# The next expert's up product ahead of the down product, combines across row groups, and the overflow branch after the eighth expert

## The chip, the core and the metric

The kernel runs on one core of a Trainium2 chip. The metric is the device time of one execution in microseconds, the median of several runs; lower is better. Engines are named as in the profile: PE is TensorE (PEld its weight loads), DVE is VectorE, ACT is ScalarE, POOL is GpSimd, and SP is the engine whose queue issues the weight loads. TensorE's clock has two levels here, 1.2 and 2.4 GHz; the profile gives the granted clock as a share of the higher one.

## The reference, cut to what matters

Two transformer blocks follow each other on 256 tokens of width 1024. The first has a mixer (mLSTM and sparse attention) and then a mixture of experts; the second has differential attention, a recurrent branch and a dense feed-forward part, twice. The change concerns the experts alone:

```python
logits = h @ w_router + b_router                 # 256 tokens, 32 experts
vals, idx = top_k(logits, 4); gate = softmax(vals)
for each expert e, for the tokens that chose it:
    up = x @ w_up[e] + b_up[e]                   # 1024 -> 2048
    glu, lin = split(up, 2)
    glu = min(glu, 7); lin = clip(lin, -7, 7)
    act = glu * sigmoid(1.702 * glu) * (lin + 1)
    out[token] += gate * (act @ w_down[e] + b_down[e])   # 1024 -> 1024
```

All of it is in fp32. The weights of one expert are 12 MiB, those of all 32 experts 403 MB; every expert is computed, with its own tokens only.

## The kernel before

**Stages.** The mixer and the router come first. At line 1131 `moe` runs the experts, `after_moe` (line 1334) normalises the sum and adds it to the residual, and `block2` (line 1473) runs the second block with weights that `load2` (line 1381) loads. The order of instructions on each engine comes from a scheduling pass, which mostly keeps program order but lets an instruction go earlier where it expects its engine to be idle.

**Slots and order.** An expert is given a fixed number of token slots. Experts 0 and 1 have 64. The others are sorted by how many tokens chose them (`sort_experts`, line 1011): four heavy ones with 96 slots, fourteen middle ones with 64, twelve small ones with 32. They run as the string `mshmmhmshmmhms` says, after 0 and 1: m is a group of two middle experts, s one of four small ones, h one heavy expert. So the ninth expert is the first heavy one, and from it on there is a run of eight: heavy, middle, middle, middle, middle, heavy, middle, middle; the same run comes once more after the next four small ones. Tokens beyond an expert's slots go to `overflow` (line 1192), four loops that run only under `tc.If(over > 0)` (line 1188); with these inputs the branch isn't taken.

**Loads.** Each expert's weights are six loads of 2 MiB, two for the up product (the glu half), two for the linear product and two for the down product. `next_w` (line 1081) puts them in turn into eight buffers, so a load waits until PE has used the load eight places before. All go through SP's queue, in program order: up, linear, down, then the next expert.

**One expert** (`expert`, line 1242). With m slots, 128/m column blocks of the weights are computed at once, each into its own 32 or 64 output rows; a heavy expert is three blocks of 32 slots. In program order on PE: transposes of the gate matrix (`ps_pg`, L1265), the up product (`ps_u`, L1278, bias L1282), the linear product (`ps_l`), the first half of the work left over from the expert before, transposes of the activations (`ps_at`, L1307; ACT copies them, L1308), the second half of that work, and the down product (`ps_d`), which ACT copies to `y` (L1319). The left-over work is the combine of the expert before and, where a group ends, the gather of the next group's tokens (`ps_g`, L1234, whose one-hot columns DVE makes at L1222 and whose result ACT scales at L1236).

**Combine** (L1326, added to `acc` by DVE at L1329). The outputs `y` lie in 128/m row groups, one for each column block; a matmul with the gate matrix of a group gives that block's columns for all tokens. There is one closure for each group (middle experts: for each group and half of the tokens), and each goes through all its matmuls, in its own accumulation bank, before the next begins. The eight banks (`ps`) serve every product, gather and transpose as well. An fp32 matmul shows as two records in the trace.

**The end.** After the last expert its combine runs, then `load2(0, 0, NW)` issues the first four loads of block 2, then comes the branch, then the other loads of block 2. `after_moe` follows with high priority: transposes of x into four banks (L1355), squares (L1346, L1347), a Newton rsqrt on DVE and a diagonal (L1360), and the matmuls at L1368; meanwhile the first weights of block 2 are split into two parts (ACT L1392, DVE L1395).

Of the kernel before, what the change touches and what calls it, by code (L numbers as in the profile page):

```python
# [19 lines left out]
P = 128  # L20
# [17 lines left out]
LEAD1 = 3  # L38
NFF = DFF // P
# [154 lines left out]
class Kernel:  # L194
# [936 lines left out]
    def moe(self):  # L1131
# [9 lines left out]
        ahead, todo = {}, []  # L1141
        with ExitStack() as s:
# [7 lines left out]
            for r in order:  # L1150
                if r == 0:
                    w = self.w01
                elif r == 1:
                    src = self.expert_chunks(1)
                    w = [self.next_w(src[c], f"we1_{c}") for c in range(6)]
                else:
                    reg = nc.sync.value_load(self.eord[0:1, r : r + 1], min_val=0, max_val=NE - 1)
                    src = self.expert_chunks(reg)
                    w = [self.next_w(src[c], f"we{r}_{c}") for c in range(6)]
                n = slots[r]  # L1160
                if r < 2:
                    col = col01[r]
                    if r == 0:
                        x01, steps = self.gather(col01, 64, "01")
                        for f in steps:
                            f()
                    xg = x01[:, :, r * 64 : r * 64 + 64]
                else:
                    col = (self.sslot[:, :, r : r + 1], self.sgate[:, :, r : r + 1], self.perm3[:, r : r + 1])
                    xg = ahead[r]  # L1170

                i = order.index(r) + 1
                if i < NE and order[i] in after and order[i] > 1:
                    g = after[order[i]]
                    m = slots[g[0]]
                    xs, steps = self.gather([(self.sslot[:, :, q : q + 1],) for q in g], m, f"{g[0]}")
                    for j, q in enumerate(g):
                        ahead[q] = xs[:, :, j * m : j * m + m]
                    todo += steps
                todo = self.expert(col, n, w, xg, f"{r}", (lambda: self.sort_experts(pm)) if r == 0 else None, todo)  # L1180
                if r == 0:
                    over = nc.values_load(self.rem[0:1, NE : NE + 1], min_val=-T1, max_val=T1)
                    self.consts2(self.kp)
            for f in todo:
                f()
            self.wx = None
            self.load2(0, 0, NW)
            with tc.If(over > 0):
                self.overflow()
            self.load2(0, NW)  # L1190

    def overflow(self):
# [5 lines left out]
        for lo, hi, cap in ((0, 2, 64), (2, 2 + NHEAVY, 96), (2 + NHEAVY, NE - NSMALL, 64), (NE - NSMALL, NE, 32)):  # L1198
            with tc.For_i(lo, hi, 1) as r:
                for b in range(-(-(T1 - cap) // 64)):  # L1200
                    rem = nc.values_load(self.rem[0:1, bass.ds(r, 1)], min_val=-T1, max_val=T1)
                    with tc.If(rem > 64 * b):
# [9 lines left out]
                        for f in self.expert((cslot, cgate, cperm), 64, w, xg, f"o{lo}_{b}"):  # L1212
                            f()
# [28 lines left out]
    def expert(self, col, n, w, xg, tag, between=None, fill=()):  # L1242
# [8 lines left out]
        per = 512 // wd  # L1251
        wide = [min(per, u - i) * wd for i in range(0, u, per)]
# [3 lines left out]
        gt = []  # L1256
        for b in range(u):
            pg = pm.tile([P, 2, P], F32, name=f"pg{tag}_{b}", tag="pg", bufs=2)
            io = self.iotas[:, b * m : b * m + m].unsqueeze(1).to_broadcast([P, q, m])
            for tt in range(2):  # L1260
                o = pg[:, tt].rearrange("p (a b) -> p a b", b=m)
                nc.vector.tensor_scalar(o, io, slot[:, tt], gate[:, tt], op0=ALU.is_equal, op1=ALU.mult)  # L1262
            ppg = self.ps(f"ps_pg{tag}_{b}")
            for tt in range(2):
                nc.tensor.transpose(ppg[:, tt * P : tt * P + P], pg[:, tt], self.ident)  # L1265
# [720 lines left out]
```

## Time and profile before

| | us |
|---|---|
| median of 3 runs | 1983.63 |
| lowest and highest of them | 1977.98, 1987.27 |
| profiled execution, its own time | 1976.5 |
| span of that execution's trace | 1974.8 |
| PE busy in the span | 1804.5 (91%) |
| DVE, ACT, POOL busy | 817.0, 572.5, 263.1 |
| mean granted TensorE clock | 0.937 |

The page's second part cuts the span into 40 slices of 49.4 us. A timeline line gives start, duration, engine, line, operation and, in brackets, how long the engine had been idle before and what ended that. A count of records can be a little low, since some matmul records are missing. A suffix q (SPq, DVEq) means the engine's sequencer: branches, semaphores and the issue of loads.

### The profile page before, as it was taken

Reading aid. Unit: us, or ns where it says so; the run is one execution under the profiler, and the core shown is the slowest. Engines: PE = TensorE matmul, PEld = TensorE weight load, DVE = VectorE, ACT = ScalarE, POOL = GpSimd, SP = SyncE. Lnnn points to the kernel's source line nnn. Section 1 sums busy time; section 2 is a strip of 40 time slices with the busy share of each in tenths; the row PEclk is TensorE's granted clock in tenths of the full one; section 3 lists DMA queues with packets and bytes.
Section 4 is the critical chain, followed back from the end, with each engine's and each line's share of the span. In section 5 each row is a group of like instructions: output and inputs, shape, how many; then the busy total and the mean of one; then the engine's idle time right before and its main releaser. Section 6 shows DMA issues by size and latency. Waiting matters only on the chain. (4 is left out here: it accounts for less than half of the span.)

```text
span 1974.8 us, 34249 instructions
## 1 busy us (share of the span) xinstructions
PE 1804.5 (91%) x14547; PEld 1282.8 (65%) x14548; DVE 817.0 (41%) x1804; ACT 572.5 (29%) x1128; POOL 263.1 (13%) x259
## 2 busy tenths in 40 slices
PE   6999979968999998699999975879999999789998
PEld 3777743435543544354345433868999999689998
DVE  3364642211212122111222222687666557876653
ACT  3454611101111101010111101345444446354442
POOL 2213110000000000000000000151233202423320
PEclk8899989987989999898999987789999999899999
DMA  9447779999999989999998899221343453225441
GB/s 386 174 190 273 294 279 429 427 427 425 427 428 428 372 367 425 427 426 428 426 427 339 369 427 399 91 86 43 129 171 144 151 209 122 86 76 186 183 147 52
DMA packets 42698, 557.73 MB, mean 282 GB/s; under 512 B 4788, under 2 KB 5964, under 8 KB 8360
## 3 DMA queue, kind: packets, MB, share of 16 engines
q1 hardware_dynamic: 39920, 548.67, 68.0%
q0 software_dynamic: 1200, 4.29, 0.6%
q10 hardware_dynamic: 1416, 2.49, 0.4%
q8 instruction: 116, 1.90, 0.4%
q14 instruction: 46, 0.38, 0.1%
HBM read 554.37 MB, written 1.06 MB: 281 GB/s over the span
## 5 line engine op out<-in xcount | busy, mean ns | idle before, releaser
L338 PE MATMUL ps_lin<-xhi,wh 128*128 128x272 f32 (+1 forms) x1024 | 301.1, 295 | 1.5 <-ACT xhi L1373 1.5
L339 PE MATMUL ps_lin<-xlo,wh 128*128 128x272 f32 (+1 forms) x1024 | 297.2, 291 | 0.9 <-DVE xlo L1374 0.9
L340 PE MATMUL ps_lin<-xhi,wl 128*128 128x272 f32 (+1 forms) x1024 | 296.8, 290 | 0.0
L1278 PE MATMUL ps_u<-we,xg 128*32 128x256 f32 (+1 forms) x2048 | 215.0, 460 | 29.1 <-DMA we<-wexp 29.1
L1278 PE MATMUL ps_d<-we,at 128*32 128x256 f32 (+1 forms) x2048 | 215.6, 457 | 14.6 <-DMA we<-wexp 11.1
L1278 PE MATMUL ps_l<-we,xg 128*32 128x256 f32 (+1 forms) x2048 | 208.7, 447 | 20.6 <-DMA we<-wexp 20.6
L338 PEld LDWEIGHTS ps_lin<-xhi,wh 128*128 128x128 f32 x1024 | 197.2, 193 | 4.0 <-ACT xhi L1373 1.7
L339 PEld LDWEIGHTS ps_lin<-xlo,wh 128*128 128x128 f32 x1024 | 196.9, 192 | 1.4 <-DVE xlo L1374 1.1
L340 PEld LDWEIGHTS ps_lin<-xhi,wl 128*128 128x128 f32 x1024 | 197.0, 192 | 0.0
L1278 PEld LDWEIGHTS ps_u<-we,xg 128*32 128x32 f32 (+1 forms) x2048 | 88.3, 122 | 137.2 <-issue 92.3
L1278 PEld LDWEIGHTS ps_l<-we,xg 128*32 128x32 f32 (+1 forms) x2048 | 88.6, 120 | 129.4 <-issue 91.3
L1278 PEld LDWEIGHTS ps_d<-we,at 128*32 128x32 f32 (+1 forms) x2048 | 87.0, 121 | 130.0 <-issue 86.2
L1326 PE MATMUL ps_c<-y,gt 32*128 32x256 f32 (+1 forms) x512 | 133.7, 494 | 0.5 <-ACT y L1319 0.5
L1349 POOL TENSOR_TENSOR hT<-hT,g 128x1024 f32<-128x1024 f32 x1 | 3.2, 3249 | 972.9 <-DVE ssm L1347 972.9
L1329 DVE TENSOR_TENSOR hT<-hT,ps_c 128x512 f32<-128x512 f32 x128 | 83.7, 685 | 118.4 <-PE ps_c L1326 118.2
L1392 ACT CAST wh<-wgu 128x1024 fp32r<-128x1024 f32 x88 | 92.2, 1049 | 122.0 <-PE ps_lin L339 119.3
L1395 DVE TENSOR_TENSOR wl<-wgu,wh 128x1024 fp32r<-128x1024 f32 x88 | 108.3, 1231 | 41.2 <-ACT wh L1392 41.0
L1290 DVE TENSOR_SCALAR gl<-ps_u 128x512 f32<-128x512 f32 (+1 forms) x36 | 20.3, 572 | 241.8 <-PE ps_u L1282 241.8
L1262 DVE TENSOR_SCALAR pg<-cols,sslot,sgate 128x128 f32<-128x128 f32 x76 | 22.5, 344 | 204.2 <-PE ps_pg L1265 204.2
L1326 PEld LDWEIGHTS ps_c<-y,gt 32*128 32x128 f32 (+1 forms) x512 | 74.7, 210 | 41.5 <-issue 31.1
L1308 ACT COPY at<-ps_at 128x512 f32<-128x512 f32 (+1 forms) x36 | 17.3, 492 | 290.2 <-PE ps_at L1307 290.2
L338 PE MATMUL ps_lin<-ahi,wh 128*128 128x272 f32 (+1 forms) x352 | 100.5, 286 | 0.0
(675 smaller groups left out, 3078.5 us busy)
## 6 DMA issues: line engine op xcount, KB each, us to landing
we<-wexp SPq DMA_DIRECT2D x192, 2048.0 KB, 17.4
wgu<-wgu SPq DMA_DIRECT2D x22, 2048.0 KB, 7.8
win<-win SPq DMA_DIRECT2D x14, 2048.0 KB, 8.3
wada<-wada SPq DMA_DIRECT2D x12, 2048.0 KB, 8.3
wdn<-wdn SPq DMA_DIRECT2D x16, 1408.0 KB, 6.2
wout<-wout SPq DMA_DIRECT2D x6, 2048.0 KB, 7.8
wint<-wint SPq DMA_DIRECT2D x2, 2048.0 KB, 11.3
wcmpNone<-wcmp SPq DMA_DIRECT2D x1, 2048.0 KB, 24.3
```

The source lines that it names most:

```text
L338: nc.tensor.matmul(po[:m, :nn], hi[:, a], xh[k], start=(k == 0), stop=False)
L339: nc.tensor.matmul(po[:m, :nn], hi[:, a], xl[k], start=False, stop=False)
L340: nc.tensor.matmul(po[:m, :nn], lo[:, a], xh[k], start=False, stop=(k == nk - 1))
L1262: nc.vector.tensor_scalar(o, io, slot[:, tt], gate[:, tt], op0=ALU.is_equal, op1=ALU.mult)
L1278: nc.tensor.matmul(dst[b][s], lhs(k, b), ws[k // 4][:, o : o + wd], start=(k == 0 and b % per == 0), stop=False)
L1290: nc.vector.tensor_scalar(gl[i], pu[i], 7.0, 0.5, op0=ALU.min, op1=ALU.mult)
L1308: nc.scalar.copy(at[i], pt[:, :x])
L1326: nc.tensor.matmul(pc[:, (tt - t0) * wd : (tt - t0) * wd + wd], gt[b][rows[s], tt * P : tt * P + P], y[b // per][rows[s], (b % per) * wd : ...
L1329: nc.vector.tensor_tensor(a, a, pc.rearrange("p (a b) -> p a b", a=per), op=ALU.add)
L1349: nc.gpsimd.tensor_tensor(u[1], acc[:, 1], self.g2, op=ALU.mult)
L1392: nc.scalar.copy(hi, src)
L1395: nc.vector.tensor_tensor(lo, src, hi.bitcast(F32), op=ALU.subtract)
```

## The change

1. `expert` returns four steps, `up`, `lin`, `down` and `combine`. The gate transposes move from ahead of the up product to ahead of the linear one.
2. `moe` runs for each expert: its linear product, the combine of the expert before, then (where a new group begins) the gather and in any case the up product of the next expert, and only then its own transposes and down product. Loads are issued in that order too: linear, next up, down.
3. In the combine the loop over row groups is the innermost one: a matmul of each group in turn, each into its own bank; the adds on DVE follow when all are issued.
4. After the eighth expert (`NBREAK = 8`) the next up product is not brought forward. The eighth expert's combine runs, the ninth's six loads are issued, and then comes the branch with `overflow` inside. The loads inside it no longer advance the ring. The ninth expert starts behind it with its gather.
5. At the end the last combine is followed by `load2(0)` whole, with no branch in between.

The sort and `consts2` (constants of block 2) come after the first expert's up product; before, the sort stood there and the constants after its down product.

```diff
-        self.nw += 1
+        self.nw += not second
...
+            xg, last = {}, None
+            for n, r in enumerate(order):
+                nxt = order[n + 1] if n + 1 < NE else None
+                if r not in steps:
+                    for f in fetch(after[r]) if r in after else []:
+                        f()
+                    up(r)
+                if n == 0:
+                    self.sort_experts(pm)
                     over = nc.values_load(self.rem[0:1, NE : NE + 1], min_val=-T1, max_val=T1)
                     self.consts2(self.kp)
-            for f in todo:
-                f()
+                weights(r, 1)
+                steps[r][1]()
+                if last is not None:
+                    steps[last][3]()
+                last = r
+                ahead = nxt is not None and n + 1 != NBREAK
+                if ahead:
+                    weights(nxt, 0)
+                    for f in fetch(after[nxt]) if nxt in after else []:
+                        f()
+                    up(nxt)
+                weights(r, 2)
+                steps[r][2]()
+                if n + 1 == NBREAK:
+
+                    steps[last][3]()
+                    last = None
+                    for i in range(3):
+                        weights(nxt, i)
+                    with tc.If(over > 0):
+                        self.overflow()
+            steps[last][3]()
             self.wx = None
-            self.load2(0, 0, NW)
-            with tc.If(over > 0):
-                self.overflow()
-            self.load2(0, NW)
+            self.load2(0)
...
+        def combine():
+            gt, y = S["gt"], S["y"]
+
+            for t0 in range(0, 2, per):
+                pc = [self.ps(f"ps_c{tag}_{t0}{s}") for s in range(q)]
                 for tt in range(t0, t0 + per):
                     for b in range(u):
-                        nc.tensor.matmul(pc[:, (tt - t0) * wd : (tt - t0) * wd + wd], gt[b][rows[s], tt * P : tt * P + P],
-                                         y[b // per][rows[s], (b % per) * wd : (b % per) * wd + wd], start=(b == 0), stop=(b == u - 1))
-                a = self.acc[:, t0 : t0 + per, s * wd : s * wd + wd]
-                nc.vector.tensor_tensor(a, a, pc.rearrange("p (a b) -> p a b", a=per), op=ALU.add)
-            return f
-
-        return [combine(s, t0) for s in range(q) for t0 in range(0, 2, per)]
+                        for s in range(q):
+                            nc.tensor.matmul(pc[s][:, (tt - t0) * wd : (tt - t0) * wd + wd], gt[b][rows[s], tt * P : tt * P + P],
+                                             y[b // per][rows[s], (b % per) * wd : (b % per) * wd + wd], start=(b == 0), stop=(b == u - 1))
+                for s in range(q):
+                    a = self.acc[:, t0 : t0 + per, s * wd : s * wd + wd]
+                    nc.vector.tensor_tensor(a, a, pc[s].rearrange("p (a b) -> p a b", a=per), op=ALU.add)
+
+        return up, lin, down, combine
```

`weights(r, i)` issues the two loads of product i of expert r, if they are not issued yet; `fetch` starts a group's gather and returns its parts; `up(r)` makes the four steps of expert r and runs the first.

## Rows read from the trace of the kernel before

**Rows 1.** The page: bytes moved in each of 40 slices of 49.4 us.

```profile
GB/s 386 174 190 273 294 279 429 427 427 425 427 428 428 372 367 425 427 426 428 426 427 339 369 427 399 91 86 43 129 171 144 151 209 122 86 76 186 183 147 52
```

**Rows 2.** Stretches: busy time by engine (instructions), then PE clock, DMA share, GB/s.

```profile
540.00:550.00 10.00, 10.00 (x31) 7.69 (x29) 1.38 (x2) 0.59 (x1) 0.00 (x0) 0.53 1.00 424
...
660.00:740.00 80.00, 80.00 (x667) 39.83 (x660) 16.21 (x30) 8.34 (x20) 0.00 (x0) 0.96 0.87 357
...
1030.00:1115.00 85.00, 85.00 (x655) 43.55 (x648) 16.42 (x28) 8.31 (x19) 0.00 (x0) 0.92 0.84 342
...
1213.00:1232.00 19.00, 10.80 (x84) 8.15 (x84) 3.67 (x7) 5.49 (x8) 0.00 (x0) 0.64 0.96 403
```

**Rows 3.** The page, DMA issues: count, KB each, us from issue to landing.

```profile
win<-win SPq DMA_DIRECT2D x14, 2048.0 KB, 8.3
```

**Rows 4.** Timeline of PE at expert 0: start, us, [idle before].

```profile
285.69 0.66 PE L1307 MATMUL ps_at<-ident,li 128*128 128x128 f32 x4 [1.51 <-DVE li L1301]
...
287.02 7.09 PE L1278 MATMUL ps_d<-we,at 128*64 128x512 f32 x32 [0.68 <-ACT at L1308]
```

**Rows 5.** Timeline of PE, from the eighth expert to the seventeenth.

```profile
467.82 1.13 PE L1326 MATMUL ps_c<-y,gt 32*128 32x256 f32 x4
...
468.88 7.07 PE L1234 MATMUL ps_g<-oh,x 128*128 128x96 f32 x32
...
479.58 0.65 PE L1265 MATMUL ps_pg<-ident,pg 128*128 128x128 f32 x4
...
506.63 3.84 PE L1234 MATMUL ps_g<-oh,x 128*128 128x128 f32 x32
...
535.91 4.69 PE L1326 MATMUL ps_c<-y,gt 32*128 32x256 f32 x24
...
541.54 9.06 PE L1326 MATMUL ps_c<-y,gt 32*128 32x256 f32 x24
...
574.29 1.98 PE L1326 MATMUL ps_c<-y,gt 64*128 64x512 f32 x6
...
576.79 1.12 PE L1326 MATMUL ps_c<-y,gt 64*128 64x512 f32 x2
...
603.54 1.98 PE L1326 MATMUL ps_c<-y,gt 64*128 64x512 f32 x4
...
677.19 10.57 PE L1278 MATMUL ps_d<-we,at 128*32 128x256 f32 x192
...
707.91 5.86 PE L1326 MATMUL ps_c<-y,gt 32*128 32x256 f32 x24
...
752.35 0.44 PE L1265 MATMUL ps_pg<-ident,pg 128*128 128x128 f32 x2
```

**Rows 6.** Timeline of all engines around the end of the expert stage.

```profile
1213.16 3.53 PE L1278 MATMUL ps_d<-we,at 128*32 128x256 f32 x32 [2.88 <-SPq L1188]
...
1217.34 1.17 PE L1326 MATMUL ps_c<-y,gt 32*128 32x256 f32 x16 [0.53 <-ACT y L1319]
...
1218.50 2.48 DVE L1329 TENSOR_TENSOR hT<-hT,ps_c 128x512 f32<-128x512 f32 x4 [9.24 <-PE ps_c L1326]
...
1225.54 5.99 PE L1355 MATMUL ps_x<-ident,x 128*128 128x128 f32 x32 [7.03 <-DVEq L1188]
...
1226.76 3.87 ACT L1392 CAST wh<-win 128x1024 fp32r<-128x1024 f32 x4
...
1230.81 1.23 DVE L1347 CUSTOM_DVE_ANT_0 xlo<-hT 128x1024 fp32r<-128x1024 f32 x1 [9.83 <-ACT wh L1392]
...
1238.02 2.07 PE L1368 MATMUL ps_x<-ssm,um 128*128 128x128 f32 x8 [6.49 <-DVE ssm L1360]
```

**Rows 7.** The branch's instructions: count, duration min/median/max in ns, first and last start.

```profile
L1188 SPq EVENT_SEMAPHORE  x7: 17/17/17, 1211.0 to 1223.8; - x7
...
L1188 PEldq COMPARE_BRANCH  x1: 6066/6066/6066, 1218.0 to 1218.0; - x1
...
L1188 DVEq EVENT_SEMAPHORE  x2: 21/21/21, 1225.4 to 1230.5; - x2
```

More of the change, by code (lines that the diff above doesn't have):

```diff
@@ new lines, in moe, with weights, fetch @@
+            srcs, ws, steps = {}, {0: self.w01}, {}
+            def weights(r, i):
+                if r not in srcs:
+                    e = r if r < 2 else nc.sync.value_load(self.eord[0:1, r : r + 1], min_val=0, max_val=NE - 1)
+                    srcs[r] = self.expert_chunks(e)
+                w = ws.setdefault(r, [])
+                if len(w) <= 2 * i:
+                    w += [self.next_w(srcs[r][c], f"we{r}_{c}") for c in (2 * i, 2 * i + 1)]
+            def fetch(g):
+                n = slots[g[0]]
+                if g == [0]:
+                    xs, todo = self.gather(col01, n, "01")
+                    both = (0, 1)
+                elif g == [1]:
+                    return []
+                else:
+                    xs, todo = self.gather([(self.sslot[:, :, q : q + 1],) for q in g], n, f"{g[0]}")
+                    both = g
+                for i, q in enumerate(both):
+                    xg[q] = xs[:, :, i * n : i * n + n]
+                return todo
@@ L1240, in gather, with expert @@
         return xg, [part(k0) for k0 in range(0, KT, per)]
-    def expert(self, col, n, w, xg, tag, between=None, fill=()):
+    def expert(self, col, n, w, xg, tag):
         nc, pm = self.nc, self.pm
@@ L1254, in expert @@
         sel = perm.to_broadcast([96, m])
[L1256 to L1265, printed above, removed]
[L1266 to L1267 removed]
         rows = [slice(i * m, i * m + m) for i in range(q)]
+        xs = lambda k, b: xg[:, k, b * m : b * m + m]
+        S = {}
         def product(lhs, ws, boff, name):
@@ L1309, in expert, with up @@
-        for f in fill[half:]:
-            f()
-        def acts(k, b):
-            o = (b % per) * wd + (k % nt) * P + m * (k // nt)
-            return at[b // per][:, o : o + m]
-        py = product(acts, w[4:6], 2048, f"ps_d{tag}")
-        y = t("y")
-        for i in range(len(wide)):
-            nc.scalar.copy(y[i], py[i])
-        def combine(s, t0):
-            def f():
-                pc = self.ps(f"ps_c{tag}_{t0}{s}")
+        def up():
+            pu = product(xs, w(0), 0, f"ps_u{tag}")
+            gl, sg = t("gl"), t("sg", 3)
+            for i in range(len(wide)):
+                nc.vector.tensor_scalar(gl[i], pu[i], 7.0, 0.5, op0=ALU.min, op1=ALU.mult)
+                nc.scalar.activation(sg[i], gl[i], AF.Tanh, scale=1.702)
+                nc.vector.scalar_tensor_tensor(sg[i], sg[i], 1.0, gl[i], op0=ALU.add, op1=ALU.mult)
+            S["sg"] = sg
@@ new lines, in down, with acts @@
+        def down():
+            at, li = t("at"), S["li"]
+            for i, x in enumerate(wide):
+                pt = self.ps(f"ps_at{tag}_{i}")
+                for c in range(x // P):
+                    nc.tensor.transpose(pt[:, c * P : c * P + P], li[i][:, c * P : c * P + P], self.ident)
+                nc.scalar.copy(at[i], pt[:, :x])
+            def acts(k, b):
+                o = (b % per) * wd + (k % nt) * P + m * (k // nt)
+                return at[b // per][:, o : o + m]
+            py = product(acts, w(2), 2048, f"ps_d{tag}")
+            y = S["y"] = t("y")
+            for i in range(len(wide)):
+                nc.scalar.copy(y[i], py[i])
```

83 lines of the change are left out of this document (26 added, 57 removed).

## The prediction

> **What bounds the kernel now.** I read the page's forty slices first, for the stage in which experts run, then a table of stretches, the page's row of loads, the timeline of PE (TensorE) through the start and one run of experts, then the tail, and last the rows of the branch. The slices show the expert stage as the plateau of some 427 GB/s in slices 7 to 24 [rows 1]. Each load of 2 MiB then takes 2.097 MB / 427 GB/s = 4.91 us, and an expert's six take 29.5 us; alone, a load of this size took 8.3 us from issue to landing, so some 3 us lie ahead of its data [rows 3]. Only less waiting by the loads, or less work outside them, can shorten this stage; PE time by itself is worth nothing here.
>
> Two holes stand in the plateau. From 660 to 740 us the loads ran at 357 GB/s, which loses (427 - 357) / 427 x 80 = 13.1 us, and from 1030 to 1115 us at 342 GB/s, which loses 16.9 us, while PE was busy for every microsecond of both [rows 2]. The eight weight buffers form a ring, so a load waits until PE has used the load eight places before it. Both holes come near the end of a run of eight experts, heavy, middle, middle, middle, middle, heavy, middle, middle. The first run lasts from 479.6 to 752.4 us, 272.8 us of PE, against 8 x 29.5 = 235.7 us of loads [rows 5]. PE falls 37.1 us behind, 13.1 us of it is lost, so the ring swallowed 24.0 us.
>
> After the last load, for which PE waited until 1213.16 us, comes a tail with no cover. The last combine ends at 1218.5 us, the adds at 1221.0, and VectorE's next instruction starts at 1230.81; PE's first block 2 work waits for that [rows 6].
>
> **The change part by part.** *Combines.* A combine's matmuls read 32 or 64 rows. The rows show how they overlap: one row group's two small matmuls (four records) took 1.13 us, four row groups' eight took 1.17 us [rows 5, 6]. At 64 rows, one column half took 1.12 us, two halves in one row group 1.98 us, and three with a change of group in between 1.98 us [rows 5]. A heavy combine has six matmuls for each row group, one group after the other: 4.69 us for two groups, and 9.06 or 5.86 us for the next two, where the granted clock fell to 0.53, the 1.2 GHz level, in the first case [rows 2, 5]. With groups interleaved I expect half of 4.69 us plus a start of some 0.4 us, 2.8 us, for all four groups of a heavy expert, 1.98 us for a middle expert instead of 3.10 or 3.96, and 1.17 instead of 2.28 for a small one. In a run of eight: two heavy combines fall from 13.75 + 10.55 to 5.6 us, minus 18.7; one small by 1.1; five middle by 1.1, 2.0, 1.1, 1.1, 1.1. Together minus 26.2 us of PE.
>
> *Order of products.* The next up product now covers VectorE's work between a linear product and its transposes, where PE had waited, 1.51 us at expert 0 [rows 4]. In exchange the transposes are followed by the down product at once, and the copy between them, formerly covered by combines and gathers, shows; its one bare instance cost PE 0.68 us [rows 4]. Bounds are 0 (transposes slip into an earlier gap) and 1.5 us; I take 0.68, or 5.4 us in a run. PE's run is then 272.8 - 26.2 + 5.4 = 252.0 us, 16.3 us behind the loads, inside the 24.0 that the ring swallows. So the second hole closes: minus 16.9 us. Only beyond about 1 us more for each expert would it open again.
>
> *Four banks at once.* A small or heavy combine now holds four of the eight accumulation banks until VectorE's adds have read them; four adds took 2.48 us [rows 6]. The linear product holds one or two, the gather two, the next up product one or two, so eight just do; I cost this at nothing. If the cover failed, PE would wait 2.48 - 1.17 = 1.3 us for each. The Trainium skill, TensorEngine Tiling (Array Packing), PSUM Bottleneck, warns that tiling speeds up TensorE but not the emptying of its banks. By that the combines gain nothing beyond the adds' pace, a run costs 8 x 1.3 = 10 us more and stands at 26 us behind, so the second hole keeps about 2 us; no row so far shows PE waiting for a bank in the runs.
>
> *Order at the start.* SP's loads go in program order, and for the first expert its down weights are already in place before the second's up product, while PE now runs that up product (7.1 + 0.4 us) first. The buffer of its first half is then free for reuse 7.5 - 1.5 (the wait that goes) - 0.4 (transposes that move) = 5.6 us later [rows 4]. The load before covers some of it: between 0 and 5.6, I take plus 3 us. The constants and the sort keep their place; they depend on nothing that moves.
>
> *The branch, removed from the tail.* PE's jump past the overflow code took 6.07 us, and VectorE's two semaphore instructions behind its own came at 1225.4 and 1230.5 us [rows 7]. VectorE stood idle 9.83 us before it went on [rows 6]. That wait is put down to ScalarE's casts, which end at 1226.76 + 3.87 = 1230.63. If they truly release it, they in turn start 4.7 us earlier (the chain ahead of them ends at 1221.0 instead of 1225.7). So the gain is 4.7 to 9.8 us. Nothing that VectorE does there reads a cast, and the late semaphore instruction stands right ahead of it: I take minus 9. What is late next is the chain on VectorE itself (7.2 us to PE's restart at 1238.02), which stays. The block 2 weights lose a queue barrier and gain nothing else: their loads were already running.
>
> *The branch, added after the eighth expert.* Queued behind it are, on VectorE, the one-hot columns of the next gather, and on PE that gather and a heavy up product, which need them. Call B the time from PE's last combine to that gather, plus what the clock costs. PE stood 7.0 us behind the old branch, and VectorE 1230.81 - 1218.51 = 12.3 us; a gather after a lull took 7.07 instead of 3.84 us [rows 5, 6], as at half the clock. B lies between 10.2 and 16; I take 14, nearer VectorE's row, as the gather needs VectorE. SP has six loads out before it jumps, 29.5 us of work, and after the old branch its last event came 12.8 us after its first, at 1223.8 [rows 7]; that is under half of 29.5, so the loads go on. Let T be the landing of the eighth expert's last load. The thirteenth load after it reuses a buffer that holds the ninth expert's down weights, and these now wait for the tenth's up product. PE gets there at T + 4 (rest and combine) + B + 3.8 + 10.9 + 12.2 (up, transposes, linear) + 3.8 + 7.4 (next gather and up) + 1.5 + 5.2 = T + 48.8 + B [rows 4, 5]; the queue needs its 3 us from issue [rows 3]. The loads are there at T + 12 x 4.91 = T + 58.9. So they stop for B - 7.1, which is 6.9 us (3.1 to 8.9). That hole replaces the first one: minus 13.1 plus 6.9. The Trainium skill, Advanced Engine Details and Errata, Control Flow Timing, gives some 108 ns for a compare-and-branch; by it B would be under 7, this hole nothing, and the sum 7 us better. The trace has 6.07 us for it on PE, and the measurement decides.
>
> **Sum**, against the profiled execution's 1976.5 us (span 1974.8): + 3 - 13.1 + 6.9 - 16.9 - 9 = -29.1 us, so 1947 us. That execution lies 7 us under the median of the runs, 1983.6; carried over to it, **1955 us**. Ends of the terms give -37 (1947) and -20 (1963).
>
> **The rivals.**
> (a) *The branch holds everything.* If every engine stays until all six loads have landed, B is 29 and the new hole 22 us; if SP issues none in that time, the queue runs dry for another 8. Sum -14 to -6: 1970 to 1978. For it: seven events on SP that spread over 12.8 us [rows 7]. Against: PE went on at 1225.54 us with block 2's loads still running at 403 GB/s [rows 2, 6]. Chance 0.13.
> (b) *Slower: banks taken early.* The block 2 transposes at L1355 need only x, have high priority, and take four banks; the branch at the end kept them behind the stage [rows 6], and nothing does so any more. Run early, they leave four banks for some twenty-four experts, each combine waits for the linear product's reader and each gather for the four adds, 1.5 + 2.5 = 4 us. A run then costs 8 x 4 = 32 us more of PE, of which the ring has 24.0 - 16.3 = 7.7 to spare; two runs lose 49 us, and the sum is + 20 us: 2004. It decides from 29 / 2 + 7.7 = 22 us in a run, 2.8 us for each expert. Against: at expert 0 PE stood 1.51 us [rows 4] with the next expert's gate transposes ready, and took nothing up from ahead. Chance 0.08.
> (c) *Interleaving does nothing*: PE's order comes out otherwise, or 32-row groups with six matmuls each still go one by one. A run stays at 272.8 + 5.4 us and the second hole grows by 5; the first grows by 5 and by B, 14. Sum + 3 + 19 + 5 - 9 = + 18: 2002. Against it stands the 1.17 us row. Chance 0.05.
>
> **How the numbers follow.** Forecast 0.74, with 1947 to 1963 and 5 us more each way for the median's own spread (1978 to 1987 in three runs). To hold 8 in 10 I add most of (a): 1942 to 1976. A difference under 0.5% (10 us) can't be told from none. Faster by more: 0.74 less a little for a sum that falls short, plus half of (a), 0.78; within: the rest of (a) and that little, 0.09; slower: (b) and (c), 0.13.
>
> **What would show it.** Right: 427 GB/s throughout the second run; one hole of 3 to 9 us some 55 to 65 us after the eighth expert's last load; heavy combines near 2.8 us; VectorE's gap after the last adds below 1 us; PE idle 8 to 13 us at the new branch. Wrong: PE waiting for accumulation banks, transposes waiting over 1 us ahead of each down product, the loads stopping at the branch itself, or the cast still setting VectorE's start.

## The result and the profile after

The changed kernel took 1952.48 us (1948.96 to 1953.55), beside 1981.74 us for the kernel before on the same chip: a ratio of 0.9856, 95% interval 0.9831 to 0.9881. The forecast was 1955 us. The profiled execution of after has a span of 1947.3 us, 27.5 us less than before's.

I split each profiled execution at three points that every kernel here has: the start of the first gather, the start of the second half of the last down product (released by the last load), and the first of the final transposes that use the diagonal (L1368 before, L1398 after). The stretch between the first two I call the loop, the next one the end.

| us | loop | end | from there on | span |
|---|---|---|---|---|
| before | 1213.16 - 261.02 = 952.1 | 24.9 | 736.8 | 1974.8 |
| after | 1189.88 - 260.05 = 929.8 | 17.3 | 740.2 | 1947.3 |

So the loop gave 22.3 us, the end 7.6 and the start of the stage 1.0; 3.4 went back later.

The page's bytes by slice, after [before: rows 1]:

```profile
GB/s 384 181 183 270 307 269 430 426 427 425 393 426 427 427 426 427 427 425 428 427 426 427 427 427 349 98 52 36 173 173 133 149 222 93 82 87 188 175 149 52
```

Both dents of before (372, 367 and 339, 369) are gone; a new, small one stands in the eleventh slice. Two stretches of after, columns as in rows 2: the new hole, and the place of the old second one.

```profile
520.00:545.00 25.00, 25.00 (x273) 11.10 (x271) 1.99 (x4) 2.64 (x7) 0.00 (x0) 1.00 0.90 358
...
1030.00:1115.00 85.00, 76.14 (x712) 34.95 (x704) 16.47 (x32) 9.24 (x23) 0.00 (x0) 0.96 1.01 427
```

The hole loses (427 - 358) / 427 x 25 = 4.0 us. In the second run of eight PE now is the one that waits, 8.9 us of 85 idle, where it was busy throughout [rows 2].

The combines in PE's timeline of after [rows 5]: a small one, a heavy one and a middle one.

```profile
460.35 1.15 PE L1356 MATMUL ps_c<-y,gt 32*128 32x256 f32 x16
...
545.01 2.87 PE L1356 MATMUL ps_c<-y,gt 32*128 32x256 f32 x48
...
571.28 1.99 PE L1356 MATMUL ps_c<-y,gt 64*128 64x512 f32 x8
```

The new branch, in the timeline of PE and then of DVE:

```profile
475.65 1.15 PE L1356 MATMUL ps_c<-y,gt 32*128 32x256 f32 x16 [0.52 <-ACT y L1346]
484.26 5.92 PE L1259 MATMUL ps_g<-oh,x 128*128 128x96 f32 x32 [7.46 <-DVE oh L1247]
...
483.78 0.57 DVE L1247 TENSOR_SCALAR oh<-cols,sslot,r2k 128x96 f32<-128x96 f32 x2 [4.48 <-DVEq L1211]
```

The branch's own instructions (columns as in rows 7):

```profile
L1211 SPq EVENT_SEMAPHORE  x7: 17/17/17, 471.3 to 492.9; - x7
...
L1211 DVEq EVENT_SEMAPHORE  x2: 21/21/21, 483.5 to 483.6; - x2
...
L1211 PEldq COMPARE_BRANCH  x1: 6083/6083/6083, 476.3 to 476.3; - x1
```

PE stands 7.46 us, and the gather behind it takes 5.92 us. VectorE's two semaphore instructions come 0.1 us apart here, and it goes on 0.2 us behind them; at the old place the two were 5.1 us apart [rows 7]. The hole comes some 50 us later, while PE is busy throughout.

The end of the stage after [rows 6]:

```profile
1189.88 1.93 PE L1293 MATMUL ps_d<-we,at 128*32 128x256 f32 x32 [1.23 <-DMA we<-wexp]
...
1192.44 0.71 PE L1356 MATMUL ps_c<-y,gt 32*128 32x256 f32 x8 [0.52 <-ACT y L1346]
1193.09 3.84 PE L1385 MATMUL ps_x<-ident,x 128*128 128x128 f32 x32
1196.86 0.71 PE L1356 MATMUL ps_c<-y,gt 32*128 32x256 f32 x8
...
1197.59 2.48 DVE L1360 TENSOR_TENSOR hT<-hT,ps_c 128x512 f32<-128x512 f32 x4 [14.54 <-PE ps_c L1356]
...
1200.19 1.22 DVE L1377 CUSTOM_DVE_ANT_0 xlo<-hT 128x1024 fp32r<-128x1024 f32 x1
...
1201.22 3.87 ACT L1422 CAST wh<-win 128x1024 fp32r<-128x1024 f32 x4
...
1207.13 2.08 PE L1398 MATMUL ps_x<-ssm,um 128*128 128x128 f32 x8 [9.56 <-DVE ssm L1390]
```

VectorE's gap of 9.83 us behind the last adds is gone: it goes on at once, ahead of ScalarE's casts. But the 32 transposes of x, which have high priority, now stand between the two halves of the last combine, and the adds wait for the second half.

### The profile page after: what moved, and what is told of

It reads as the page before. It is cut to its first block, busy times and chain, and to the rows that moved or that the text cites. A ratio compares the mean times of both kernels' runs of the same rounds, so it can differ in the third digit from the quotient of the medians.

```text
span 1947.3 us, 34253 instructions
## 1 busy us (share of the span) xinstructions
PE 1746.0 (90%) x14547; PEld 1239.9 (64%) x14548; DVE 811.6 (42%) x1804; ACT 570.7 (29%) x1128; POOL 264.4 (14%) x259
## 4 chain that ended last, share of the span: by engine, by line
PE 56%; DMA 12%; DVE 5%; ACT 1%; issue 1%; ACTq 0%; POOL 0%; DVEq 0%; POOLq 0%
DMA we<-wexp 12%; PE ps_lin L339 9%; PE ps_lin L340 9%; PE ps_lin L341 9%; PE ps_l L1293 6%; PE ps_u L1293 6%; PE ps_d L1293 6%; PE ps_g L1259 2%; PE ps_c L1356 2%; DVE qk L1765 1%; PE ps_at L1336 1%; PE nm0ss L1473 0%; PE ps_rqb L1784 0%; PE ps_ri L1659 0%; PE ps_pg L1321 0%
## 5 line engine op out<-in xcount | busy, mean ns | idle before, releaser
L1293 PE MATMUL ps_d<-we,at 128*32 128x256 f32 (+1 forms) x2048 | 219.7, 475 | 47.6 <-DMA we<-wexp 38.1
L1293 PE MATMUL ps_l<-we,xg 128*32 128x256 f32 (+1 forms) x2048 | 214.0, 454 | 30.6 <-DMA we<-wexp 29.7
L1293 PE MATMUL ps_u<-we,xg 128*32 128x256 f32 (+1 forms) x2048 | 211.9, 452 | 29.1 <-DMA we<-wexp 29.1
L1360 DVE TENSOR_TENSOR hT<-hT,ps_c 128x512 f32<-128x512 f32 x128 | 79.3, 682 | 131.7 <-PE ps_c L1356 131.7
L341 PE MATMUL ps_lin<-ahi,wl 128*128 128x272 f32 (+1 forms) x352 | 99.9, 284 | 0.0
L340 PE MATMUL ps_lin<-alo,wh 128*128 128x272 f32 (+1 forms) x352 | 99.8, 283 | 0.0
L1422 ACT CAST wh<-win 128x1024 fp32r<-128x1024 f32 (+1 forms) x72 | 60.9, 855 | 117.9 <-PE ps_lin L340 115.2
## 6 DMA issues: line engine op xcount, KB each, us to landing
wcmpNone<-wcmp SPq DMA_DIRECT2D x1, 2048.0 KB, 22.7
```

What stands on the lines that cost most here:

```text
L340: nc.tensor.matmul(po[:m, :nn], hi[:, a], xl[k], start=False, stop=False)
L341: nc.tensor.matmul(po[:m, :nn], lo[:, a], xh[k], start=False, stop=(k == nk - 1))
L1293: nc.tensor.matmul(dst[b][s], lhs(k, b), ws[k // 4][:, o : o + wd], start=(k == 0 and b % per == 0), stop=False)
L1360: nc.vector.tensor_tensor(a, a, pc[s].rearrange("p (a b) -> p a b", a=per), op=ALU.add)
L1422: nc.scalar.copy(hi, src)
```

## The experiments

Three theories. Theory 1, mine: the loads bound the loop, and the combine across row groups takes TensorE's backlog out of the runs of eight, so the loads no longer stop. Theory 2: the new order of the products does it. Theory 3: the place of the branch does it. The three edits can each be done alone, so seven combinations besides before were run. Then come one-place edits. Times of runs are given as a ratio to the kernel before on the same chip, with its 95% interval; loop and end are those of the profiled execution.

**The combine alone** (before's code, one matmul of each group in turn; half of the tokens ahead of the activation's transposes, half behind, but both ahead where a gather follows):

```diff
-        def combine(s, t0):
+        def combine(tt):
...
+                for b in range(u):
+                    for s in range(q):
+                        nc.tensor.matmul(pc[s][...], gt[b][rows[s], ...], y[b // per][rows[s], ...], ...)
...
-        return [combine(s, t0) for s in range(q) for t0 in range(0, 2, per)]
+        return [combine(0), combine(1)]
```

> The kernel before with one edit: an expert's combine is issued with the row group innermost, into as many banks at once as there are row groups. Product order and branch stay as they were. Theory 1 (the combine gives the gain: it takes TensorE's backlog out of the heavy runs, so the loads no longer stop): both stretches below 427 GB/s in the middle of the expert loop close, 13.1 and 16.9 us, and the last expert's combine is some 1.5 us shorter; 26 to 33 us faster than before, the heavy combines at 2.8 us each and VectorE's gap of 9.8 us at the end still there. Theory 2 (the new order of the products gives the gain, by covering waits): 0 to 5 us faster. Theory 3 (moving the branch gives it): 0 to 3 us faster.

Measured: 1952.58 us, 0.9868 (0.9812 to 0.9923). Loop 929.9, end 18.8. Its page shows not one dent:

```profile
GB/s 387 175 179 267 293 262 417 427 427 427 426 427 428 426 428 426 428 426 427 427 426 427 427 428 312 124 64 25 172 170 136 149 222 92 82 87 187 176 149 52
```

This edit alone gives what the whole change gives. Theory 1 holds as far as it goes. Two things that I had expected didn't come. A heavy combine takes 1.99 + 1.57 = 3.6 us in its two pieces instead of 2.8, and VectorE's gap at the end is 3.78 us instead of 9.8, though the branch stands where it was. So 6.1 us of the gain lie at the end (24.9 to 18.8), and no run shows why.

**The product order alone** (after's code with the combine of before and the branch at the end):

```diff
-            for t0 in range(0, 2, per):
-                pc = [self.ps(f"ps_c{tag}_{t0}{s}") for s in range(q)]
+            for s in range(q):
+                for t0 in range(0, 2, per):
+                    pc = self.ps(f"ps_c{tag}_{t0}{s}")
...
-                if n + 1 == NBREAK:
...
+            self.load2(0, 0, NW)
+            with tc.If(over > 0):
+                self.overflow()
+            self.load2(0, NW)
```

> The kernel after with two edits undone: each combine goes bank by bank as before, and the branch is back behind the last expert. What is left is the new order of the products. Theory 1: no gain; some 3 us later at the start, and a copy of 0.68 us bare ahead of a down product deepens the backlog of the heavy runs by up to 5 us each, so the two holes stay at 13 and 17 us or grow; 0 to 15 us slower than before, 8 the likeliest. Theory 2: 15 to 25 us faster. Theory 3: within 3 us of before.

Measured: 1959.44 us, 0.9904 (0.9876 to 0.9933). Loop 932.6, end 22.7. I had expected it slower by 8 us; it is some 19 faster. Here theory 1 as I had put it fell: two different edits each take away most of the same holes. The page shows what is left of them:

```profile
GB/s 386 183 184 271 307 264 428 427 427 426 427 427 429 425 393 426 426 427 427 428 426 369 424 427 358 130 64 24 173 173 133 149 222 94 80 87 189 173 149 52
```

All the combines' matmuls over the stage, from a table of one stretch by tile (columns: length, then PE, PEld and DVE busy with counts, clock, DMA share, GB/s), first for before:

```profile
290.00:1240.00 950.00, 133.72 (x512) 74.68 (x512) 83.75 (x128) 0.93 0.97 409
```

The product order alone:

```profile
290.00:1240.00 950.00, 97.50 (x512) 61.03 (x512) 80.64 (x128) 0.92 0.97 411
```

The combine alone:

```profile
290.00:1240.00 950.00, 64.04 (x512) 31.52 (x512) 79.84 (x128) 0.94 0.98 413
```

After:

```profile
290.00:1240.00 950.00, 60.20 (x512) 30.55 (x512) 79.29 (x128) 0.93 0.97 412
```

With the new order the combines cost 36.2 us less though they still go bank by bank. The timeline of that kernel shows why: a heavy one takes 11.64 us, within the 10.55 to 13.75 of before (4.69 + 5.86 and 4.69 + 9.06 [rows 5]), but a middle one takes 1.99 us, as little as across groups.

```profile
531.26 11.64 PE L1351 MATMUL ps_c<-y,gt 32*128 32x256 f32 x48
...
568.01 1.99 PE L1351 MATMUL ps_c<-y,gt 64*128 64x512 f32 x8
```

A heavy combine that goes bank by bank also costs something behind its end. The granted clock falls in it, though PE is busy throughout: to 0.53 in before, the 1.2 GHz level [rows 2], and to a mean of 0.68 here from 540 to 550 us. The product behind it then takes 8.92 us in before and 8.80 here; in after, where the clock stays at 1.00, it takes 7.09. The lines are of before, then two of the product order alone, then two of after:

```profile
550.53 8.92 PE L1278 MATMUL ps_d<-we,at 128*64 128x512 f32 x32
...
540.00:550.00 10.00, 10.00 (x33) 4.00 (x34) 0.75 (x2) 0.00 (x0) 0.00 (x0) 0.68 1.00 426
...
542.84 8.80 PE L1288 MATMUL ps_u<-we,xg 128*64 128x512 f32 x32
...
540.00:550.00 10.00, 10.00 (x84) 4.67 (x82) 3.48 (x6) 0.00 (x0) 0.00 (x0) 1.00 1.02 433
...
547.82 7.09 PE L1293 MATMUL ps_u<-we,xg 128*64 128x512 f32 x32
```

The new order has the combine in one piece; before, the activation's transposes cut it in two, and a row group that was left alone behind them ran without a partner (1.98 + 1.12 us, or twice 1.98 [rows 5]). The next kernel tests that.

**The combine in one piece, all else as before:**

```diff
-        return [combine(s, t0) for s in range(q) for t0 in range(0, 2, per)]
+        whole = [combine(s, t0) for s in range(q) for t0 in range(0, 2, per)]
+        return [lambda: [f() for f in whole]]
...
-        half = len(fill) // 2
+        half = 1
```

> The kernel before with one edit: an expert's combine, still bank by bank with a row group after the other, is issued in one piece ahead of the next activation's transposes instead of in two pieces around them. Products and branch stay. It tells why the new product order alone made the loop 19.5 us shorter (952.1 to 932.6 us). If that was the combine in one piece (its matmuls took TensorE 97.5 us instead of 133.7), the combine takes some 97 us here too and the loop 931 to 938 us, the whole some 15 to 20 us less than before. If it was the new order, by the waits that it covers, the combine takes some 130 us and the loop stays at 948 to 955.

Measured: 1963.5 us, 0.9900 (0.9865 to 0.9936). Loop 934.5, end 24.3, and the combines:

```profile
290.00:1240.00 950.00, 91.46 (x512) 56.04 (x512) 80.75 (x128) 0.92 0.98 413
```

So 17.6 of the 19.5 us that the product order gave the loop are the combine in one piece; what the order covers besides is worth at most 2 us, less than the 2.9 us by which the loops of two executions of after differ (929.8 and 932.7).

**The branch alone** (before's code; `load(order[8])` is the ninth expert's six loads):

```diff
+                if i == 8:
+                    for f in todo:
+                        f()
+                    todo = []
+                    load(order[i])
+                    with tc.If(over > 0):
+                        self.overflow()
...
-            self.load2(0, 0, NW)
-            with tc.If(over > 0):
-                self.overflow()
-            self.load2(0, NW)
+            self.load2(0)
```

> The kernel before with one edit: the overflow's branch, with the six loads of the next expert ahead of it, follows the eighth expert. Products and combines stay as they were. Theory 1: the end gains the 7 to 9 us that the branch cost there, and the jump's 9.6 us come on top of the first run's backlog, so the first hole grows from 13 to some 20 to 23 us; within 4 us of before. Theory 2: the same. Theory 3: 15 to 25 us faster.

Measured: 1977.69 us, 1.0006 (0.9981 to 1.0031): no change. Loop 960.5, end 15.9. The end gained 9.0 us, as forecast, and the loop lost 8.4. Theory 3 falls. The page has a new dent early in the first run (370), and the old one there is deeper (397 and 309 in place of 372 and 367), by slices 23.7 us in place of 13.3; the second run loses a little less than before (369, 361):

```profile
GB/s 384 176 184 271 295 275 423 426 428 423 427 370 427 397 309 427 426 425 428 429 427 369 361 426 427 155 83 43 129 171 147 162 211 105 86 78 182 184 147 52
```

PE stood 8.30 us at the branch, so where the ring has nothing to spare, nearly all of the jump is paid.

**After with the old combine** (product order and branch):

```diff
-            for t0 in range(0, 2, per):
-                pc = [self.ps(f"ps_c{tag}_{t0}{s}") for s in range(q)]
+            for s in range(q):
+                for t0 in range(0, 2, per):
+                    pc = self.ps(f"ps_c{tag}_{t0}{s}")
```

> The kernel after with one edit undone: each combine goes bank by bank, a row group after the other, as before. Theory 1: the second hole is back with 17 to 22 us and the first grows to 20 to 25 us; 25 to 45 us slower than after, that is, from 3 us faster to 16 slower than before. Theory 2: within 8 us of after. Theory 3: within 8 us of after.

Measured: 1962.16 us, 0.9910 (0.9887 to 0.9934). Loop 946.1, end 15.9. 16 us of loop more than after, where I had expected 25 to 45 us in all: the edit of the combine is needed to pay for the branch, but the combine in one piece has already closed part of the holes.

**After with the branch at the end** (product order and combine):

```diff
-                if n + 1 == NBREAK:
...
+            self.load2(0, 0, NW)
+            with tc.If(over > 0):
+                self.overflow()
+            self.load2(0, NW)
```

> The kernel after with one edit undone: the branch is back behind the last expert, with four of the next stage's loads ahead of it. The new product order and the combine across row groups stay. Measured from the first gather's start to the start of the last down product's second half (929.8 us after, 952.1 before) and from there to the final transposes of the stage that follows (17.3 after, 24.9 before). Theory 1 (the loads bound the loop; the moved branch costs only the hole of 4.0 us and gives the end back what it cost there): the loop takes some 926 us with no stretch below 427 GB/s, the end 19 to 25; 2 us faster to 4 slower than after. Theory 3 (the branch's place matters by itself): 10 us or more slower than after.

Measured: 1952.32 us, 0.9851 (0.9821 to 0.9881). Loop 926.9 and no stretch below 427 GB/s, end 20.2. Moving the branch is worth nothing in after: 3.0 us given at the end, 2.9 taken in the loop.

**Combine and branch, products in their old order:**

```diff
+        def combine(tt):
...
+                if i == 8:
+                    for f in todo:
+                        f()
+                    todo = []
+                    load(order[i])
+                    with tc.If(over > 0):
+                        self.overflow()
```

> The kernel before with two of the three edits: the combine across row groups, and the branch behind the eighth expert with the next expert's six loads ahead of it. The products keep their old order. Theory 1: the combine alone leaves so much spare time on TensorE that the branch's jump opens a hole of no more than 4 us; the loop takes 930 to 934 us, the end some 16; within 4 us of after, so that the new product order is worth nothing once the combine goes across row groups. Theory 2 (the product order is needed): 8 to 20 us slower than after.

Measured: 1950.11 us, 0.9836 (0.9798 to 0.9873). Loop 928.0, end 18.9. No hole shows, though the branch stands at the same place as in after; the end is 2.9 us longer than I had expected. Theory 2 falls: beside the combine the product order is worth nothing. Its timeline at the branch:

```profile
472.58 3.71 PE L1239 MATMUL ps_g<-oh,x 128*128 128x96 f32 x32
...
481.52 1.15 PE L1336 MATMUL ps_c<-y,gt 32*128 32x256 f32 x16 [0.52 <-ACT y L1324]
490.94 1.17 PE L1270 MATMUL ps_pg<-ident,pg 128*128 128x128 f32 x4 [8.27 <-DVE pg L1267]
```

The ninth expert's gather runs here ahead of the branch, in 3.71 us; in after it runs behind it, in 5.92. That this is why no hole opens here wasn't tested.

The loop, in one table (us):

| | branch at the end | branch after the eighth |
|---|---|---|
| old order, old combine | 952.1 | 960.5 |
| new order, old combine | 932.6 | 946.1 |
| old order, new combine | 929.9 | 928.0 |
| new order, new combine | 926.9 | 929.8 |

Each is one execution; a second one of after has 932.7.

**After without the branch** (it and the overflow's work are left out):

```diff
                     for i in range(3):
                         weights(nxt, i)
-                    with tc.If(over > 0):
-                        self.overflow()
```

> The kernel after without the branch and what it guards (the overflow's work is left out); the eighth expert's combine still stands ahead of the next expert's gather. If the jump makes the hole of 4.0 us, the hole is gone and the loop takes some 926 us instead of 929.8. The rival: the hole comes from the order at this place, the next up product and its gather not being ahead, and stays.

Measured: 1944.58 us, one execution; loop 927.1, end 17.3. The hole is gone, so the branch made it. The edit takes PE's jump and SP's stop away together; that PE is busy in all 25 us of the hole speaks for the jump. The timeline at that place:

```profile
474.82 1.15 PE L1354 MATMUL ps_c<-y,gt 32*128 32x256 f32 x16 [0.52 <-ACT y L1344]
475.89 3.81 PE L1257 MATMUL ps_g<-oh,x 128*128 128x96 f32 x32
```

The same gather takes 3.81 us. So the branch costs PE 7.46 us of standing and 5.92 - 3.81 = 2.1 us of a slower gather: 9.6 us.

**The branch after the fourth expert:**

```diff
-NBREAK = 8
+NBREAK = 4
```

> The kernel after with one number changed: the branch follows the fourth expert, behind which four experts of 32 rows come, instead of the eighth, behind which a heavy expert of 96 rows comes. Theory 1 (the hole is the jump of TensorE on top of the heavy expert's backlog): the hole of 4.0 us is gone, since the experts of 32 rows take less TensorE time than their loads; 3 to 5 us faster than after. The rival (the hole is SyncE's stop at the branch): the hole stays, some 55 us behind the branch; no change.

Measured: 1949.77 us, 0.9838 (0.9810 to 0.9867). Loop 928.9, end 17.2. The hole didn't go; a smaller one stands right behind the branch:

```profile
370.00:400.00 30.00, 20.78 (x272) 15.38 (x272) 8.96 (x28) 4.06 (x11) 0.00 (x0) 0.83 0.96 389
```

It loses (427 - 389) / 427 x 30 = 2.7 us. My expectation looked only at the experts behind the branch. Four experts of 64 slots stand ahead of this one, and PE comes to it with no time in hand (the first four down products don't wait for a load). The rival isn't borne out either: SP's own events end at 370.5 us, and in the waits of its loads (engine, line, what it waited for: us in total, times, longest) the longest is one for PE's up product; it ends near 389 us, in the middle of the hole (385 to 395 us):

```profile
SPq L1092 <- PE ps_u L1293: 11.8, 1, 11.8
```

So what decides seems to be how far PE is behind when it stops; no run varied that alone.

**The transposes of x behind the last combine:**

```diff
-            steps[last][3]()
+            self.lastc = steps[last][3]()
...
-        for k in range(KT):
-            for tt in range(2):
-                ...
+        with self.tc.issue_after(self.lastc):
+            for k in range(KT):
+                for tt in range(2):
+                    ...
```

> The kernel after with one edit: the 32 transposes of x that the next stage issues with high priority are queued behind the last expert's combine, instead of between its two halves. If they delay the last adds by their 3.84 us, the end shrinks from 17.3 to some 13.5 us and the kernel is 3 to 4 us faster than after. The rival: VectorE's and ScalarE's chain to the diagonal sets the final transposes whatever the combine does, and nothing changes.

Measured: 1947.13 us, 0.9823 (0.9794 to 0.9853). Loop 929.3, end 13.3: 4.0 us less, the whole price of the transposes.

```profile
1195.31 1.93 PE L1293 MATMUL ps_d<-we,at 128*32 128x256 f32 x32 [1.20 <-DMA we<-wexp]
...
1197.88 1.15 PE L1356 MATMUL ps_c<-y,gt 32*128 32x256 f32 x16 [0.52 <-ACT y L1346]
1198.95 3.84 PE L1387 MATMUL ps_x<-ident,x 128*128 128x128 f32 x32
1208.58 2.08 PE L1400 MATMUL ps_x<-ssm,um 128*128 128x128 f32 x8 [5.79 <-DVE ssm L1392]
```

**Combine, branch and late transposes, products in their old order, and after once more beside it:**

```diff
+                if i == 8:
...
             for f in todo:
-                f()
+                self.lastc = f()
...
+        with self.tc.issue_after(self.lastc):
```

> The kernel before with the combine across row groups, the branch behind the eighth expert, and the 32 high-priority transposes of x behind the last combine; the products keep their old order. If the parts add up, the loop takes 928 us as without the late transposes, the end some 13.3 instead of 18.9: 1 to 7 us faster than after.

> The kernel after, unchanged, beside the others on the same chip: as it ran, 0.983 to 0.988 of before.

Measured: 1945.20 us, 0.9799 (0.9767 to 0.9831), loop 926.9, end 13.3; after 1949.93 us, 0.9831 (0.9796 to 0.9865), loop 932.7, end 17.2. The parts add up. By the medians it is 4.7 us ahead of after and 35 of before; the intervals of the two ratios overlap, so over after the profile's loop and end speak for it, not the runs alone.

## Why the prediction was right, and where not

The sum of -29.1 us met a difference of 27.5 us in the spans and 29.3 us in the medians. By its terms:

- *What bounds the stage*: right. Every kernel without a dent has a loop of 926.9 to 929.9 us, whichever of the edits it has.
- *Second hole, -16.9*: right; 427 GB/s and PE idle for 8.9 us there.
- *First hole, -13.1*: right, it is closed.
- *Combine, -26.2 us in a run of eight*: the sizes were right (2.87, 1.99 and 1.15 us against 2.8, 1.98 and 1.17). Interleaving the groups does it alone: 69.7 of the 73.5 us over the stage (64.04 us in place of 133.72). But I took it for the only way. The combine in one piece, bank by bank, gives 42.3 us (91.46), and it is part of the reordering, which gives 36.2 (97.50). The gains overlap; beside the one piece, interleaving is needed for the heavy experts alone, 48 records each. The row of three matmuls in 1.98 us with a change of group in between [rows 5] had hinted at it: two groups ran side by side there without interleaving. The term also lacked the slower product behind a heavy combine: 8.92 and 9.26 us in before's first run against 7.09 in after, 4.0 us more in a run.
- *Order of products, +5.4*: over-sized. The copy is bare for 12 experts of 32, 8.3 us in all the stage; behind four of the first run's five gathers the scheduling pass put the transposes inside the next up product, my bound of 0. Four of the run's eight are bare, 0.73 us each, 2.9 us. Against them stand 2.2 us in which PE waited for VectorE ahead of the transposes in before's run, and no longer does. And that the order shortens the combines had no term at all; alone it is worth 19.5 us of loop.
- *Four banks at nothing*: held. DVE's adds stayed at 79.29 us (83.75 before) and no wait of PE for a bank shows in the runs. The Trainium skill's warning (TensorEngine Tiling (Array Packing), PSUM Bottleneck), that tiling speeds up TensorE but not the emptying of its banks, is not what decides here: the adds are spread over 900 us and have cover.
- *Start, +3*: wrong. The stretches of 60 us from the first gather, before and after, move bytes at the same rate. The table of stretches of before:

```profile
261.02:321.02 60.00, 57.15 (x304) 26.32 (x306) 16.32 (x57) 10.16 (x25) 0.00 (x0) 0.97 0.99 401
```

And of after:

```profile
260.05:320.05 60.00, 58.66 (x306) 26.64 (x308) 15.68 (x55) 10.24 (x25) 0.00 (x0) 0.94 0.98 401
```

  The lower bound, 0, was the right value. Yet the loop gave 22.3 us where the holes gave 30.0 - 4.0 = 26.0. Where the other 3.7 lie isn't settled; over the whole loop after moved some 2.4 us more of data than before (423 GB/s x 929.8 us against 412 x 952.1, each to about 1 us), which would be loads of the next stage.
- *New hole, +6.9*: right in kind. It came to 4.0 us in one execution of after and 7.4 in the other. The row of the other:

```profile
530.00:555.00 25.00, 25.00 (x310) 12.49 (x304) 3.37 (x6) 1.77 (x4) 0.00 (x0) 1.00 0.75 300
```

  B was mis-sized: 14 against 7.46 + 2.1 = 9.6 in the first, below my lower bound of 10.2, and against 7.60 + 3.3 = 10.9 in the other, where the gather took 7.12 us. I had sized it by VectorE's 12.3 us behind the old branch, and VectorE doesn't stand that long at the new one. The 7.1 us that I set against B was too large as well (9.6 - 7.1 = 2.5, measured 4.0). The two errors partly cancel. The Trainium skill (Advanced Engine Details and Errata, Control Flow Timing) has 108 ns for a compare-and-branch; PE's took 6083 ns here, and without the branch the loop is 2.7 us shorter, so the measurement was the one to go by.
- *End, -9*: -7.6. Where only the branch moved, the end fell by 9.0, and VectorE's gap went as said; in after it starts ahead of the casts. But the reason that I gave for the gap in before, the late second semaphore [rows 7], isn't borne out. With the product order alone the two lie 0.1 us apart, and VectorE still stands 9.32 us, until ScalarE's casts end (1204.21 + 3.87 = 1208.08); with the combine alone (last line) it stands 3.78 us:

```profile
L1208 DVEq EVENT_SEMAPHORE  x2: 21/21/21, 1202.8 to 1202.9; - x2
...
1208.13 1.23 DVE L1371 CUSTOM_DVE_ANT_0 xlo<-hT 128x1024 fp32r<-128x1024 f32 x1 [9.32 <-ACT wh L1416]
...
1205.02 1.23 DVE L1354 CUSTOM_DVE_ANT_0 xlo<-hT 128x1024 fp32r<-128x1024 f32 x1 [3.78 <-issue]
```

  What holds VectorE behind a branch at the end stays open. Over the five kernels that have it there, the end took 18.8 to 24.9 us, so what its removal is worth is known no better than that. The transposes at L1355, which rival (b) feared in the whole loop, came early for one expert, the last, and cost 4.0 us there. They did so as PE's work ahead of the last adds, not by the banks that they hold, so (b) was right that nothing held them back, and wrong in the cost.
- *Not foreseen*: 3.4 us more from the final transposes to the end of the kernel. That stretch was 734.8 to 740.3 us over all the runs; its cause wasn't tried.

Rival (a) didn't happen: SP's events ran until 492.9 us, 19.8 us behind PE's start on the eighth expert's last load, inside the 29.5 us that were out. Rival (c) didn't either.

The prediction was right in its time because the sum went by holes and the load rate: the two old holes, 30.0 us, are more than the whole difference. That it came within 1.6 us of the spans' difference is luck. It had the start 3 us and the new hole 2.9 us too dear and lacked the 1.0 us gained ahead of the first gather; against that, it had 1.4 us too much gain at the end and lacked the 3.7 us that the loop and the 3.4 us that the stretch behind the end took back. For the order alone it would have been wrong: it gave that nothing, and alone that takes 19 us.

## What to carry to other kernels

Where a stage is bound by loads, an edit is worth the holes that it closes, and two edits that close the same hole don't add up; measure each alone before crediting one. Small matmuls in different row groups want to be issued side by side, a matmul of each group in turn. Where they go group by group instead, a cut in two costs about as much as that order does: without the cut alone 42.3 of the 73.5 us came back. Interleaved, a cut matters little (64.04 us against 60.20). A high-priority block that loses its barrier goes ahead of something; look for what stands last on the critical path and queue the block behind that.

## What the runs showed of the hardware

Row groups that were issued one after the other still overlapped where each had four records in a row: two groups at 64 rows took 1.99 us bank by bank and across groups alike, four at 32 rows 1.17 and 1.15 us. With twelve records each, four groups at 32 rows took 11.64 us bank by bank and 2.87 across; part of that is the clock, which fell in the first case and not in the second. At full clock, two such groups took 4.69 us [rows 5]. Between four and twelve nothing was measured.

While PE stood at the branch the granted clock fell to 0.5, the 1.2 GHz level (0.50 from 480 to 484 us in after). In the stretch of the gather behind it the clock was 0.61 in one execution of after and 0.50 in the other:

```profile
484.00:490.00 6.00, 5.74 (x32) 5.77 (x32) 2.27 (x10) 0.84 (x3) 0.00 (x0) 0.61 1.00 418
...
489.00:496.00 7.00, 7.00 (x36) 6.83 (x40) 1.89 (x8) 1.72 (x5) 0.00 (x0) 0.50 0.98 411
```

The gather took 5.92 us in the one and 7.12 in the other, and the first 24 records of the next up product 1.50 and 2.79 us. With 0.14 us more of standing that makes 2.6 of the 3.4 us by which the two holes differ (4.0 and 7.4).

Much of the scatter between executions comes from ahead of all that changed here. Of the 7.3 us between the spans of two executions of after, 4.4 lie ahead of the first gather (260.05 and 264.43 us). Over all these kernels, one or two executions each, it started between 256.2 and 266.1 us. The quickest to get there was the kernel with the branch after the fourth expert; its stretch from 80 to 120 us:

```profile
80.00:120.00 40.00, 39.18 (x294) 31.47 (x294) 20.93 (x78) 19.81 (x59) 8.98 (x8) 0.98 0.41 158
```

The slowest was the kernel with the late transposes alone:

```profile
80.00:120.00 40.00, 39.15 (x251) 31.45 (x252) 16.55 (x61) 14.96 (x44) 7.70 (x7) 0.81 0.41 158
```

PE is as busy, but the clock was granted at 0.98 in one and 0.81 in the other, and 294 against 251 matmuls got done. A comparison of two kernels by one execution each should start from the first gather.
